# Gate columns placed anew around the S5 branch's outer products, V and states, and four blocks' sums of squares on another engine, in a decoder step on one Trainium2 core

## The chip, the cores and the metric

The kernel runs on one core of one Trainium2 chip. The metric is the time of one execution on the device in microseconds (us). TensorE is PE in the profile, its weight load PEld, VectorE is DVE, ScalarE is ACT, GpSimd is POOL, SyncE is SP.

## The reference, cut to what matters

One layer of a hybrid decoder is computed for 2048 prompt positions and for 8 sequences of 4 new positions each. Its first half is what matters here:

```python
xn = _rmsnorm(h, norm_mix[l])
proj = jnp.einsum('btd,de->bte', xn, w_in[l])          # 1024 -> 3072
u_pool = proj[..., :POOL_WIDTH]                        # 512
u_ssm = proj[..., POOL_WIDTH:POOL_WIDTH + SSM_WIDTH]   # 512
gates = jax.nn.sigmoid(proj[..., POOL_WIDTH + SSM_WIDTH:])   # 2 x 1024
a_out = _pool_mixer(hist[l], u_pool, ...)
y_ssm, s_re_last, s_im_last = _s5_mixer(u_ssm, ...)    # 32 groups, 64 complex states, a scan over time
z = jax.nn.gelu(y_ssm)
b_out = z * jax.nn.sigmoid(z @ glu_w + glu_b)
merged = gates[0] * (a_out @ w_branch_pool) + gates[1] * (b_out @ w_branch_ssm)
h = h + merged @ w_out
h = h + SwiGLU(RMSNorm(h))
```

## The kernel before, in words

All large products are made of three float16 matmuls for each pair of operands split into a high and a low part (`mm3`, lines 117 to 119). The projection's output is cut into chunks of 256 rows. A **column** is what one step of `chunk` issues: 24 matmuls for 128 output rows and 512 or 272 positions (five columns, three of 512 and two of 272, make 128 rows; ten make a chunk), ACT's evacuation out of PSUM (L363 or L366), and the DMA of the column before. Four PSUM buffers (`mm`) serve the columns, two others (`s5`) serve S5.

**`norm_in`** (from L198) normalizes the 17 blocks of input rows. `norm` takes the sum of squares of each row (L229, on ACT with a sum output), the inverse root on DVE (`rstd_of`, L61 to L72), and the split into high and low parts; `put_part` transposes these on PE (L137). Weight preparation stands beside it (`Win.prep`): a square on ACT (L89), a product on DVE (L96, or L92 where a column stands between), for the first weights two small matmuls (L98, L100), ten small DVE operations (L103 to L179) and eight splits (L52 on ACT, L53 on DVE). Blocks 0 and 1 are taken singly, blocks 2 and 3 together, and later blocks in pairs while the first columns run.

**The S5 stage** has four units of eight groups. `S5.run` is a generator; whatever it yields, a number n of columns is issued at that place (a bare yield is one). The order of instructions on each of PE, DVE, ACT and POOL is the program's here (`manual_schedule`). For each unit `un`:

- `states` (L686): for each of eight groups a matmul of V and U (L693) and two copies out of PSUM (L696), by ACT and by DVE, into R.
- `tmat` (L661): ACT copies TT into T (L666), DVE makes the outer products O (`outer`, L621: lines 626 and 629, three operations).
- `load` (L672): SP fetches the next unit's U.
- `vmat` of the next unit (L631): the outer products VT on DVE; eight transposes of VT (L641) in two PSUM buffers, each copied into V by ACT (L642); eight small matmuls (L645) whose result ACT copies into M (L648); DVE adds the diagonal into M (L383, `m<-m,dd`); SP stores M into TT.
- `scan` (L709): a scan over time of R, all on DVE (L705, L707, L737), with eight columns between its parts.
- `outputs` (L750): DVE and ACT fill S (L759, L761, L757); then columns; then for each group two matmuls (L766 with T, L767 with S) and ACT's copy into Y (L768), in two halves of four groups with a column behind each, one more column at the end, and the store of Y.

Each column of a chunk also carries a step of the preparation of the next chunk's weights, by its number k in the chunk: 1 the square, 3 the product and POOL's maximum, 7 the ten small operations, 8 and 9 four splits each (for the first chunk, 0 to 4 finish chunk 1, 5 to 9 are for the next).

Behind S5, Pool takes 13 columns, `Branch.weights` 5, then 4; the first GLU tile's preparation is issued, 5 more columns, the GLU's matmuls and all columns that are left (`put(100)`); then `merge_tile` runs for eight tiles, with the next tile's GLU issued after four of its eight steps. There the framework's scheduler orders the instructions, and it lays Pool's matmuls in the midst of columns. 100 columns exist in all.

Of the kernel before, what the change touches and what calls it, by code (L numbers as in the profile page):

```python
# [13 lines left out]
AF = mybir.ActivationFunctionType  # L14
OP = mybir.AluOpType
# [40 lines left out]
def rstd_of(E, ss, n, w=128):  # L56

    nc = E.nc
    t = E.small.tile([128, 4, n], F32, tag=f"rs{n}", name="rs")
    v, y, a, h = (t[:w, i] for i in range(4))  # L60
    nc.vector.tensor_scalar(v, ss, 1.0 / D, EPS, op0=OP.mult, op1=OP.add)  # L61
    nc.vector.tensor_scalar(h, ss, -0.5 / D, -0.5 * EPS, op0=OP.mult, op1=OP.add)  # L62
    nc.vector.tensor_scalar(a.bitcast(I32), v.bitcast(I32), 1, None, op0=OP.logical_shift_right)  # L63
    nc.vector.tensor_scalar(y.bitcast(I32), a.bitcast(I32), -1, 0x5F3759DF, op0=OP.mult, op1=OP.add)  # L64
    for _ in range(3):
        if n == 1:
            nc.vector.tensor_scalar(a, y, y, h, op0=OP.mult, op1=OP.mult)  # L67
            nc.vector.tensor_scalar(y, a, 1.5, y, op0=OP.add, op1=OP.mult)  # L68
            continue
        nc.vector.tensor_tensor(a, y, y, op=OP.mult)  # L70
        nc.vector.tensor_tensor(a, a, h, op=OP.mult)
        nc.vector.scalar_tensor_tensor(y, a, 1.5, y, op0=OP.add, op1=OP.mult)  # L72
    return y
# [67 lines left out]
class Win:  # L141


    def __init__(self, E, ctx, w_in, g):
# [7 lines left out]
        self.wp = ctx.enter_context(E.tc.tile_pool(name="wpart", bufs=3))  # L152
        self.R, self.W = {}, {}

    def load(self, c, half=None):
        if c not in self.R:
            self.R[c] = self.raw.tile([128, KB, 256], F32, name="wr")
        n = slice(0, 256) if half is None else slice(half * 128, half * 128 + 128)
        w = self.w[:, c * 256:(c + 1) * 256].rearrange("(k p) f -> p k f", p=128)
        self.E.nc.sync.dma_start(self.R[c][:, :, n], w[:, :, n])  # L160

    def prep(self, c, ps=None, half=None):

        E, nc, t = self.E, self.E.nc, self.R[c]
        if c not in self.W:
# [32 lines left out]
def norm_in(E, ps, win, x_p, x_s, xh, xl, u_d, s5):  # L198

    nc, tc = E.nc, E.tc  # L200
    with ExitStack() as ctx:
        ld = ctx.enter_context(tc.tile_pool(name="xld", bufs=5))
        wk = ctx.enter_context(tc.tile_pool(name="xwk", bufs=2))
        X = {}
# [18 lines left out]
        def norm(bs):  # L223

            w = BLK[bs[0]][1]
            ss = E.small.tile([128, len(bs)], F32, tag=f"ss{len(bs)}", name="ss")
            for i, b in enumerate(bs):
                sq = wk.tile([128, D], BF16, name="sq", bufs=1)
                nc.scalar.activation(sq[:w], X[b][:w], AF.Square, accum_out=ss[:w, i:i + 1])  # L229
            yield  # L230
            r = rstd_of(E, ss[:w], len(bs), w)
            rs = E.small.tile([128, len(bs)], F32, tag=f"rx{len(bs)}", name="rx")
            nc.vector.tensor_scalar(rs[:w], r, SX, None, op0=OP.mult)
            yield
            for i, b in enumerate(bs):
                hi, lo = norm_parts(E, wk, X.pop(b), w, rs[:w, i:i + 1])
                n0 = BLK[b][0]
                T[b] = [partial(put_part, E, ps, nc.scalar.copy, hi, w, xh, n0, "tp"),
                        partial(put_part, E, ps, nc.vector.tensor_copy, lo, w, xl, n0, "s5")]
                yield  # L240
# [37 lines left out]
        g, w = norm([0]), win.prep(2, ps, 0)  # L278
# [9 lines left out]
        g, w = norm([1]), win.prep(2, ps, 1)  # L288
# [10 lines left out]
        g, w = norm([2, 3]), win.prep(3, ps)  # L299
# [12 lines left out]
        w = None  # L312
        for p in range(8):
            bs = [2 * p + 4, 2 * p + 5] if p < 6 else [16] if p == 6 else []
            nb = [b for b in (2 * p + 2, 2 * p + 3) if p and b < 16]
            g = norm(bs) if bs else iter(())
# [11 lines left out]
            n0, w = (p * 256, 256)  # L328
            if p == 7:
                w = 288  # L330
# [115 lines left out]
class S5:  # L446
# [184 lines left out]
    def vmat(self, un):  # L631
        E, nc, ps, mp = self.E, self.E.nc, self.ps, self.mats
        G = slice(un * 8, un * 8 + 8)
        VT = mp.tile([128, 8, L, HD], F32, name="vt", tag="vt")
        self.outer(VT, self.PV[:, :, :, G], self.BT[:, :, G])
        yield 2 if un < 3 else 1
        V = mp.tile([128, 8, 128], F32, name="v5")
        for h in range(2):
            p = ps.tile([128, 512], F32, name="mm", tag="s5", bufs=2)
            for g in range(4):  # L640
                nc.tensor.transpose(p[:, g * 128:(g + 1) * 128], VT[:, h * 4 + g].rearrange("p j h -> p (j h)"), E.id32)  # L641
            nc.scalar.copy(V[:, h * 4:h * 4 + 4].rearrange("p g m -> p (g m)"), p)  # L642
        p = ps.tile([128, 512], F32, name="mm", tag="s5", bufs=2)
        for g in range(8):
            nc.tensor.matmul(p[:, g * HD:(g + 1) * HD], VT[:, g].rearrange("p j h -> p (j h)"),  # L645
                             self.CT[:, 0, un * 8 + g], start=True, stop=True)
        M = mp.tile([128, 8, HD], F32, name="m5")
        nc.scalar.copy(M.rearrange("p g h -> p (g h)"), p[:, :128])  # L648
        dd = mp.tile([128, 8, HD], F32, name="dd")
        hi = slice(96, 128)  # L650
        tt(E, dd[hi], self.dv[hi, G][:, :, None].to_broadcast([32, 8, HD]),
           E.id32[hi, None, 112:128].to_broadcast([32, 8, HD]), OP.mult)
        tt(E, M[hi], M[hi], dd[hi], OP.add)
        TT = mp.tile([128, L, 8, HD], F32, name="tt5", tag="vt")
        nc.gpsimd.memset(TT, 0.0)
        for t in range(L):
            nc.sync.dma_start(TT[0:HD * (t + 1), t], M[HD * (L - 1 - t):128])
        self.M[un] = (V, TT)
        yield 0
# [26 lines left out]
    def states(self, un):  # L686

        E, nc, ps, wk = self.E, self.E.nc, self.ps, self.wk
        V, U = self.M[un][0], self.U[un]
        R = [wk.tile([128, 4, UC], F32, name=f"r{i}") for i in range(2)]  # L690
        for g in range(8):
            p = ps.tile([128, 512], F32, name="mm", tag="s5", bufs=2)
            nc.tensor.matmul(p[:, :UC], V[:, g], U[:, g], start=True, stop=True)  # L693
            e = (g % 2) * 64
            for i in range(2):
                (nc.vector.tensor_copy if i else nc.scalar.copy)(R[i][e:e + 64, g // 2], p[i * 64:i * 64 + 64, :UC])  # L696
        return R

    def cmul_add(self, un, k, o, x, a):
# [50 lines left out]
    def outputs(self, un, a):  # L750
        E, nc, ps, wk = self.E, self.E.nc, self.ps, self.wk
        pr = slice(un * 4, un * 4 + 4)
        T, O = self.M.pop(un)
        U = self.U.pop(un)
        S = wk.tile([128, 8, YC], F32, name="st5")
        nc.gpsimd.memset(S[:, :, 0:1], 0.0)
        nc.scalar.copy(S[:, :, NC:], self.S0[:, un * 8:un * 8 + 8])  # L757
        for i in range(2):
            nc.vector.tensor_copy(self.fin[:, i, 0, pr], a[i][:, :, NC - 1])  # L759
            for e in range(2):  # L760
                nc.vector.tensor_copy(S[i * 64:i * 64 + 64, e::2, 1:NC], a[i][e * 64:e * 64 + 64, :, 0:NC - 1])  # L761
        yield (3, 2, 2, 4)[un]
        Y = wk.tile([128, 8, YC], F32, name="y5")
        for g in range(8):
            p = ps.tile([128, 512], F32, name="mm", tag="s5", bufs=2)
            nc.tensor.matmul(p[:, :YC], T[:, g].rearrange("p t h -> p (t h)"), U[:, g, :YC], start=True, stop=False)  # L766
            nc.tensor.matmul(p[:, :YC], O[:, g].rearrange("p t h -> p (t h)"), S[:, g], start=False, stop=True)  # L767
            nc.scalar.copy(Y[:, g], p[:, :YC])  # L768
            if g % 4 == 3:
                yield  # L770
        nc.vector.tensor_reduce(self.ymx[:, un:un + 1], Y.rearrange("p g c -> p (g c)"), axis=AX.X, op=OP.max,
                                apply_absolute_value=True)
        o = self.y_d.offset + un * 128 * NT
        dst = lambda c, n: bass.AP(tensor=self.y_d.tensor, offset=o + c, ap=[[NT, HD], [HD * NT, 8], [1, n]])
        for t in range(L):
            nc.sync.dma_start(dst(t * NC, NC), Y[HD * t:HD * t + HD, :, 0:NC])
            if t < 4:
                nc.sync.dma_start(dst(NP_ + 8 * t, 8), Y[HD * t:HD * t + HD, :, NC:])
        yield
# [18 lines left out]
    def run(self):  # L798
        self.U = {}
        self.load(0)  # L800
        yield from self.vmat(0)
        for un in range(4):
            R = self.states(un)
            yield min(un, 1)
            yield from self.tmat(un)
            if un < 3:
                self.load(un + 1)
                yield from self.vmat(un + 1)
            yield from self.scan(un, R)
            yield from self.outputs(un, R)  # L810
        self.finish()
        yield
# [1030 lines left out]
```

## Time and profile before

| | us |
|---|---|
| median of 3 runs (2407.16 to 2411.3) | 2409.38 |
| the profiled execution's own time | 2412.55 |
| its span, first to last instruction | 2410.5 |
| PE busy | 2297.5 |
| DVE busy | 1657.8 |
| ACT busy | 1027.0 |

The mean granted clock of TensorE over the span is 0.982 of full speed (2.4 GHz). A row of the timeline gives start and length in us, the engine, the line, the operation and its tiles (out<-in), and in brackets the time that the engine sat idle before it and what ended that.

### The profile page before, as it was taken

Reading aid. Unit: us, or ns where it says so; the run is one execution under the profiler, and the core shown is the slowest. Engines: PE = TensorE matmul, PEld = TensorE weight load, DVE = VectorE, ACT = ScalarE, POOL = GpSimd, SP = SyncE. Lnnn points to the kernel's source line nnn. Section 1 sums busy time; section 2 is a strip of 40 time slices with the busy share of each in tenths; the row PEclk is TensorE's granted clock in tenths of the full one; section 3 lists DMA queues with packets and bytes.
Section 4 is the critical chain, followed back from the end, with each engine's and each line's share of the span. In section 5 each row is a group of like instructions: output and inputs, shape, how many; then the busy total and the mean of one; then the engine's idle time right before and its main releaser. Section 6 shows DMA issues by size and latency. Waiting matters only on the chain. (4 is left out here: it accounts for less than half of the span.)

```text
span 2410.5 us, 43285 instructions
## 1 busy us (share of the span) xinstructions
PE 2297.5 (95%) x16971; PEld 1616.3 (67%) x16971; DVE 1657.8 (69%) x4011; ACT 1027.0 (43%) x1867; POOL 384.5 (16%) x428
## 2 busy tenths in 40 slices
PE   6989999999999999997999999999999989988998
PEld 5866555555678874555888888888888754433543
DVE  6757757838568778776555565555555688789877
ACT  6633232244334433455445454444454552243332
POOL 0000000000000000000121121211121345454342
PEclk8999999999999999998999999999999999999999
DMA  6232332255334343323122121221222344444332
GB/s 208 81 91 81 76 99 76 76 165 185 127 112 130 111 132 137 140 75 123 54 80 79 63 80 54 80 88 54 80 70 72 119 144 159 135 170 142 123 125 79
DMA packets 200529, 257.50 MB, mean 107 GB/s; under 512 B 23798, under 2 KB 161334, under 8 KB 199805
## 3 DMA queue, kind: packets, MB, share of 16 engines
q1 hardware_dynamic: 179813, 228.73, 30.6%
q10 hardware_dynamic: 20480, 25.83, 3.0%
q8 instruction: 132, 2.16, 0.4%
q14 instruction: 72, 0.59, 0.1%
q0 software_dynamic: 32, 0.18, 0.0%
HBM read 167.03 MB, written 86.67 MB: 105 GB/s over the span
## 5 line engine op out<-in xcount | busy, mean ns | idle before, releaser
L974 PEld LDWEIGHTS <-W 128*128 128x128 f16 x7392 | 726.0, 98 | 115.8 <-issue 15.6
L974 PE MATMUL p<-m,W 128*128 128x256 f16 (+1 forms) x3084 | 356.6, 275 | 1.5 <-ACT v L1006 1.5
L118 PE MATMUL mm<-xl,wh 128*128 128x512 f16 (+4 forms) x1072 | 348.2, 325 | 1.6 <-DVE xl L138 1.6
L117 PE MATMUL mm<-xh,wh 128*128 128x512 f16 (+4 forms) x1072 | 348.3, 325 | 0.0
L119 PE MATMUL mm<-xh,wl 128*128 128x512 f16 (+4 forms) x1072 | 348.0, 325 | 0.0
L117 PE MATMUL pd<-m,W 128*128 128x512 f16 x616 | 235.4, 382 | 19.2 <-ACT xr L1222 5.5
L119 PE MATMUL pd<-m,W 128*128 128x512 f16 x616 | 234.5, 382 | 1.6 <-DVE W L383 1.6
L118 PE MATMUL pd<-m,W 128*128 128x512 f16 x616 | 235.2, 382 | 0.0
L974 PE MATMUL p<-x,W 128*128 128x256 f16 x1848 | 205.7, 273 | 3.6 <-ACT p L995 2.8
L974 PE MATMUL p<-xq,W 128*128 128x256 f16 x1764 | 199.8, 275 | 5.5 <-ACT p L995 4.1
L1007 POOL TENSOR_TENSOR p<-v,p 128x256 f32<-128x256 f32 (+1 forms) x88 | 71.3, 811 | 668.2 <-ACT v L1006 522.9
L383 DVE TENSOR_TENSOR w<-u,p 128x272 f32<-128x272 f32 (+1 forms) x86 | 36.5, 424 | 172.6 <-PE p L974 169.3
L119 PEld LDWEIGHTS <-wl 128*128 128x128 f16 x1072 | 106.8, 100 | 68.6 <-issue 3.1
L118 PEld LDWEIGHTS <-wh 128*128 128x128 f16 x1072 | 106.9, 100 | 66.4 <-issue 0.6
L117 PEld LDWEIGHTS <-wh 128*128 128x128 f16 x1072 | 107.4, 100 | 65.3 <-issue 0.6
L1220 POOL TENSOR_TENSOR xq<-xq,xr 128x512 f32<-128x512 f32 x90 | 128.7, 1450 | 42.0 <-DVE xq L1221 17.3
L366 ACT ACTIVATE go<-mm,wc 128x512 f32<-128x512 f32 (+1 forms) x80 | 48.3, 604 | 181.8 <-PE mm L119 176.5
L118 PEld LDWEIGHTS <-W 128*128 128x128 f16 x616 | 60.5, 98 | 93.1 <-issue 22.7
L119 PEld LDWEIGHTS <-W 128*128 128x128 f16 x616 | 60.6, 98 | 76.2 <-DVE W L383 2.8
L117 PEld LDWEIGHTS <-W 128*128 128x128 f16 x616 | 60.6, 98 | 74.1 <-issue 2.2
L1006 ACT COPY v<-p 128x272 f32<-128x272 f32 (+1 forms) x86 | 32.1, 374 | 168.0 <-PE p L974 160.9
L117 PE MATMUL po<-woh,m 128*128 128x512 f16 x256 | 97.0, 379 | 0.9 <-DVE x L383 0.9
(474 smaller groups left out, 4404.2 us busy)
## 6 DMA issues: line engine op xcount, KB each, us to landing
f_d<-m SPq DMA_DIRECT2D x44, 512.0 KB, 3.3
xq<-f_d SPq DMA_DIRECT2D x40, 512.0 KB, 4.5
x<-in_x_prompt_dram SPq DMA_DIRECT2D x32, 512.0 KB, 4.5
xq<-h_d SPq DMA_DIRECT2D x32, 512.0 KB, 4.1
g<-g_d SPq DMA_DIRECT2D x56, 256.0 KB, 2.8
g_d<-go ACTq DMA_DIRECT2D x48, 256.0 KB, 2.0
gr<-in_ffn_w_gate_dram SPq DMA_DIRECT2D x23, 512.0 KB, 4.2
ur<-in_ffn_w_up_dram SPq DMA_DIRECT2D x23, 512.0 KB, 5.1
```

The lines of the kernel that those rows point to most:

```text
L117: nc.tensor.matmul(q, ah, bh, start=first, stop=False)
L118: nc.tensor.matmul(q, ah, bl, start=False, stop=False)
L119: nc.tensor.matmul(q, al, bh, start=False, stop=last)
L366: nc.scalar.activation(o[:, :w], q[:, :w], AF.Tanh, scale=cc[:, 1:2])
L383: E.nc.vector.tensor_tensor(o, a, b, op=op)
L974: nc.tensor.matmul(q, W[:, x, a, ka], X[b][:, y, k, :w], start=begin and k == v == 0, stop=end and k == 3 and v == 2, skip_group_check=True)
L1006: nc.scalar.copy(v, x)
L1007: nc.gpsimd.tensor_tensor(p5, v, p5, op=OP.add)
L1220: add = (lambda o, x: tt(E, o, o, x, OP.add)) if end else (lambda o, x: nc.gpsimd.tensor_tensor(o, o, x, op=OP.add))
```

## The change

In `vmat` three columns instead of two (one in the last unit) stand between the outer products and V's transposes, and a new column stands between V's copies and the matmuls of L645. `states` becomes a generator with a column after its fourth group; the column that stood behind the states of units 1 to 3 goes. In `outputs` 2, 1, 2 and 4 columns instead of 3, 2, 2 and 4 stand ahead of the matmuls of Y in units 0 to 3. In `norm_in` the sums of squares of blocks 0 to 3 are taken by DVE, as a product of the block with itself with a sum output, instead of by ACT.

```diff
             for i, b in enumerate(bs):
                 sq = wk.tile([128, D], BF16, name="sq", bufs=1)
-                nc.scalar.activation(sq[:w], X[b][:w], AF.Square, accum_out=ss[:w, i:i + 1])
+                if b < 4:
+                    nc.vector.scalar_tensor_tensor(sq[:w], X[b][:w], 1.0, X[b][:w], op0=OP.mult, op1=OP.mult,
+                                                   accum_out=ss[:w, i:i + 1])
+                else:
+                    nc.scalar.activation(sq[:w], X[b][:w], AF.Square, accum_out=ss[:w, i:i + 1])
...
         self.outer(VT, self.PV[:, :, :, G], self.BT[:, :, G])
-        yield 2 if un < 3 else 1
+        yield 3
...
             nc.scalar.copy(V[:, h * 4:h * 4 + 4].rearrange("p g m -> p (g m)"), p)
+        yield 1
         p = ps.tile([128, 512], F32, name="mm", tag="s5", bufs=2)
...
                 (nc.vector.tensor_copy if i else nc.scalar.copy)(R[i][e:e + 64, g // 2], p[i * 64:i * 64 + 64, :UC])
+            if g == 3:
+                yield 1
         return R
...
-        yield (3, 2, 2, 4)[un]
+        yield (2, 1, 2, 4)[un]
...
         for un in range(4):
-            R = self.states(un)
-            yield min(un, 1)
+            R = yield from self.states(un)
             yield from self.tmat(un)
```

## Rows read from the trace of the kernel before

**Rows 1.** The page's part 1: busy us (share of the span) and instructions.

```profile
PE 2297.5 (95%) x16971; PEld 1616.3 (67%) x16971; DVE 1657.8 (69%) x4011; ACT 1027.0 (43%) x1867; POOL 384.5 (16%) x428
```

**Rows 2.** Busy time by stage; columns: stretch, us, five engines' busy, clock, DMA, GB/s.

```profile
142.40:508.40 366.00, 345.84 (x1854) 204.09 (x1853) 255.96 (x976) 113.81 (x230) 8.47 (x23) 0.97 0.32 86
...
680.50:900.00 219.50, 211.43 (x1875) 183.83 (x1873) 174.46 (x393) 97.44 (x173) 1.08 (x3) 0.99 0.42 123
```

**Rows 3.** Waits of PE in the S5 stage: us in total, times, longest.

```profile
PE mm L693 <- DVE r L696: 6.2, 10, 2.1
PE mm L645 <- ACT v L642: 3.1, 3, 2.5
PE mm L693 <- DMA u<-u_d: 3.0, 1, 3.0
...
PE mm L766 <- ACT y L768: 2.3, 2, 1.2
```

**Rows 4.** Timeline of PE: states of unit 1, V, S of unit 2, states of unit 3.

```profile
253.65 1.20 PE L693 MATMUL mm<-u,v 128*128 128x272 f32 x4 [0.60 <-DVE r L696]
...
270.88 1.28 PE L641 MATMUL mm<-id,vt 128*128 128x128 f32 x8 [1.94 <-DVE vt L629]
...
404.25 0.79 PE L767 MATMUL mm<-st,o 128*128 128x264 f32 x2 [2.84 <-DVE st L761]
...
429.04 1.20 PE L693 MATMUL mm<-u,v 128*128 128x272 f32 x4 [2.13 <-DVE r L696]
```

**Rows 5.** Busy time of two stretches, with the granted clock in the third last place.

```profile
271.60:278.40 6.80, 6.78 (x27) 4.61 (x25) 3.12 (x15) 1.38 (x3) 0.96 (x1) 0.50 0.66 99
...
158.95:165.80 6.85, 6.51 (x12) 3.17 (x12) 2.22 (x5) 1.89 (x5) 0.00 (x0) 0.50 0.35 82
```

**Rows 6.** Timeline of ACT: a square of the preparation, evacuations of three neighbouring columns.

```profile
385.67 1.90 ACT L89 ACTIVATE wh<-wr 128x2048 bf16<-128x2048 f32 x1
...
393.05 0.49 ACT L366 ACTIVATE go<-mm,wc 128x272 f32<-128x272 f32 x1 [2.09 <-DMA g_d<-go]
...
395.82 0.49 ACT L366 ACTIVATE go<-mm,wc 128x272 f32<-128x272 f32 x1 [2.10 <-PE mm L119]
...
401.00 0.69 ACT L366 ACTIVATE go<-mm,wc 128x512 f32<-128x512 f32 x1 [4.69 <-PE mm L119]
```

**Rows 7.** Groups of DVE in S5, shapes apart: count, busy us, mean ns, idle.

```profile
L629 DVE TENSOR_TENSOR vt<-vt,t 128x1024 f32<-128x1024 f32 x4 | 4.9, 1225 | 0.1
```

**Rows 8.** Timeline of DVE in unit 1, from the addition into M to S.

```profile
276.11 0.29 DVE L383 TENSOR_TENSOR m<-m,dd 32x128 f32<-32x128 f32 x1 [3.47 <-ACT m L648]
...
306.10 0.15 DVE L103 TENSOR_SCALAR pr<-pr 128x1 f32<-128x1 f32 x1
...
307.63 0.14 DVE L179 TENSOR_SCALAR wc<-pw 128x1 f32<-128x1 f32 x1
...
315.75 1.67 DVE L53 SCALAR_TENSOR_TENSOR wl<-wr,gs,wh 128x256 f16<-128x256 f32 x4
...
319.02 1.41 DVE L761 COPY st<-r 64x1020 f32<-64x1020 f32 x2
```

**Rows 9.** The tail: timeline of DVE, and L117's instructions (first and last start).

```profile
632.70 1.28 DVE L53 SCALAR_TENSOR_TENSOR zl<-y,bk,zh 128x1024 f16<-128x1024 f32 x1
...
656.08 0.48 DVE L53 SCALAR_TENSOR_TENSOR bl<-bt,bk,bh 128x256 f16<-128x256 f32 x1 [0.58 <-ACT bh L52]
...
661.91 0.69 DVE L1504 SCALAR_TENSOR_TENSOR y<-gq,y 128x512 f32<-128x512 f32 x1 [0.69 <-ACT gq L1503]
...
667.05 1.28 DVE L53 SCALAR_TENSOR_TENSOR zl<-y,bk,zh 128x1024 f16<-128x1024 f32 x1 [1.22 <-ACT zh L52]
...
L117 PE MATMUL mm<-zh,gluh x128: 269/273/448, 648.6 to 865.5; 128*128 128x256 f16 x112, 128*128 128x288 f16 x16
```

**Rows 10.** Timeline of DVE at the start of `norm_in`.

```profile
18.56 0.16 DVE L96 TENSOR_TENSOR pr<-pr,gmx 128x1 f32<-128x1 f32 x1 [1.39 <-ACT wh L89]
...
31.08 0.16 DVE L96 TENSOR_TENSOR pr<-pr,gmx 128x1 f32<-128x1 f32 x1 [3.84 <-ACT wh L89]
```

## The prediction, made before the result was known

> **What bounds the kernel now.** I read the page's busy times first: TensorE (PE) is busy for 95% of the span and no other engine passes 70% [rows 1]. So the table by stage comes next, to find where PE is not busy. In the S5 stage it misses 20.2 us of 366, in the merge stage 8.1 of 219.5 [rows 2]. The table of waits then names what PE waits for inside S5: the state copies 6.2, V 3.1, the load of U 3.0, S 2.8, the copies of Y 2.3 [rows 3], and PE's timeline shows each in its place [rows 4]. Last, the granted clock: after several of these waits it falls from 2.4 to 1.2 GHz, as in the 6.8 us behind the wait of 1.94 [rows 5]. The matmuls are the same before and after. The time therefore changes by PE's waits and half-clock stretches alone, and a column is worth something only as cover: one of 512 takes 5.18 us, one of 272 2.78 (evacuations of neighbouring columns start that far apart, [rows 6]).
>
> **Where the columns go.** I numbered the columns by the generator's steps. A column n has 272 positions when n mod 5 is 3 or 4, and weight preparation of the next chunk hangs on n mod 10 (1: a square on ACT; 3: a reduction; 7: ten small DVE operations; 8 and 9: four splits each on ACT and DVE). The change issues 74 columns in S5 instead of 66. Between V's last matmul (L645) and the first Y of units 0 to 3 stood 11, 10 and 10 columns, and in unit 3, which prepares no V, 13 behind the states; now it is 10, 9, 10 and 12.
>
> **V: a gain of 12 us.** V's transposes get three columns instead of two or one behind the outer products, and L645 gets one behind the copies of V. The outer products are two sets of three operations of 1.22 [rows 7], so they end some 8 us after the last state copy; the three columns last 10.7 to 15.5, so the wait of 1.94 goes [rows 4], and the copies of V, which made PE wait 3.1 in all [rows 3], lie beside the new column. That is 5.5 with two small waits for vt. A half-clock stretch goes with each of the two large ones: 6.8 us at 0.50 with PE busy for 6.78 of them [rows 5] have lost 3.4. I take 6.4 for both, since V's transposes were through before.
>
> **U: a gain of 5 us.** The first states now come two columns (7.96 us) later, past U's landing: 3.0 idle [rows 3], and the states behind that wait no longer run at half clock (0.50 over 6.85 us, [rows 5]). Those would lose 3.4, but the copies set the pace of part of them; estimate 2.0.
>
> **States: a loss of 2.6 us.** A half of four groups waits once, about 0.6, where eight groups wait three times [rows 4]; that saves 0.6 in each of four units. But what stands in ACT's and DVE's queues ahead of the copies matters more. Unit 3 of before shows it: its last column ahead of the states has n mod 10 of 8, and with four splits (1.67 on DVE, [rows 8], as much on ACT) in front of the copies the wait is 2.13 instead of 0.5 [rows 4]. The new placement puts splits ahead of the second half of unit 0 and of both halves of unit 2, and a square of 1.9 (the row at L89, [rows 6]) ahead of unit 1's first half: 3 x 1.6 + 2.0 = 6.8 against the 1.6 that goes from unit 3. Net 5.2 lost, 2.6 after the saving.
>
> **S: a loss of 11 us, the largest term.** DVE works in order, and the scan is written behind the addition into M, which waits for L645 (3.47 idle, [rows 8]). In unit 1 from that addition at 276.11 to the last copy into S at 320.43 DVE took 44.3, of which 1.6 were the ten small operations and 1.6 the splits [rows 8]: the bare chain is 41.1, and 40.4 to the part that the first Y needs (the last copy of 0.7 is for another). The addition starts 0.34 after L645. Now the cover after the change. Unit 0: 6 x 5.18 + 4 x 2.78 = 42.2, and 0.45 for Y's first matmul; preparation 1.7, chain 0.34 + 40.4 + 1.7 = 42.4: about even, 0.5 lost because splits stand ahead of the copy of M. Unit 1: 5 x 5.18 + 4 x 2.78 = 37.0, and 0.45; preparation is 1.6 + 1.6 + 1.6 + 0.1 = 4.9, the chain 45.6: PE waits 8.1. Unit 2: 42.2 against 45.5, as before, where the same count gives the measured wait of 2.84 [rows 4]; it stays. Unit 3: 6 x 5.18 + 6 x 2.78 = 47.8, and 0.45, against 1.1 to the last state copy, 3.6 for one set of outer products, 40.1 and 3.3 of preparation = 48.1: even. So 8.6 more idle, and behind the wait of 8 the half clock, which loses up to 3.4 in a stretch like those of [rows 5] and half of that in a shorter one: I take 2.5.
>
> **Y: nothing.** The waits for Y's copies (2.3, [rows 3]) come from squares ahead of them. They go, and splits ahead of three other halves cost about 1.0 each.
>
> **New half-clock stretches: a loss of 3 us.** The four lengthened state waits are of 2.1 to 2.6. Of two such waits before, 1.94 was followed by half clock and 2.13 was not. At even odds and some 1.7 each that is 3, between 0 and 7.
>
> **The tail: a loss of 4 us.** Pool and Branch take 13, 5, 4 and 5 columns as before, so the eight columns come off the end: the seven behind the first GLU matmuls, 26.6 us, are gone, and one of the five ahead of them. From the pool's end 13 columns remain, 53 us; zl stood ready at 634.0 [rows 9], 46 us after the pool's end at 588, so the first GLU still does not wait. But the seven columns hid the last bl, which ends 8.0 after the GLU's start at 648.6, and the second tile's zl, 19.7 after it [rows 9]. Without them PE has the GLU (48 matmuls of 256, 5.2 at the rate of a column of 272) and, before the second GLU, four merges (24 each, 10.5). If nothing else is put there, PE waits 1.4 for bl and some 6 for zl, since DVE must also do four merges. This part is ordered by the framework's scheduler, which can put the next four merges first; then 1 to 2 stay. I take 4, with 0 and 8 as ends.
>
> **Squares on DVE: nothing.** DVE stood idle for 1.39 and 3.84 us ahead of L96 [rows 10], exactly where the squares of block 1 and of blocks 2 and 3 now lie. No row shows a DVE multiply with a sum output; the nearest, the multiply of two f32 tiles over 512 elements, took 0.69 [rows 9], so about 1.25 for 1024. Block 1: the square ends when ACT's square did, with ACT's own next square a microsecond earlier, so L96 stays within 0.1. Blocks 2 and 3: 2.5 into 3.84 idle. Block 0 runs before the weights land. I take 0, with -0.3 and +0.5 as ends. The Trainium skill (Vector Engine (DVE) Microarchitecture Reference, section 7, Points that are easy to get wrong) says that this operation with two sources in SBUF that are not bf16 runs at half throughput; the row of 0.69 for 512 f32 elements speaks against it here. By the rule the four squares would take an estimated 2.3 each, and the sum would be 1.8 us worse.
>
> **The sum.** Against the profiled execution (2412.55, its span 2410.5): 12 + 5 - 2.6 - 11 - 3 - 4 = -3.6, so 2416.2. That execution is 3.2 above the median of 2409.38; against the median it is 2413. A measurement of this kernel tells about 0.2% (4.8 us) from no change.
>
> **The rivals.**
> Faster: the scan does not wait in unit 1. The gain of 17 at V and U is in the rows, and the loss at S is counted, not seen. If DVE's chain there ended within the cover, say because M's addition came earlier than I place it, 10 us of loss fall away, and with a tail of 2: 2409.4 - 9 = about 2400. For it speaks that units 0 and 3 come out even within half a microsecond; against it that the same count reproduces all waits for S of before.
> Slower: the second GLU tile. The place is zl of the second tile; if the scheduler holds the order GLU after four merges, as all the later tiles have it, PE waits 7.5 in all and the clock falls behind it (up to 3.4): 11 instead of 4, 2420. It decides from the point at which zl comes more than 10.5 us after the GLU's end; alone it came 14.4 after. With the other end of the half-clock term 2424.
> No effect: the gains are eaten earlier than I think and the scheduler fills the tail: 2409, within 2.
>
> **How the numbers follow.** The forecast of 2413 gets 0.42 (its own range 2409 to 2418), the faster rival 0.20, the slower 0.25, no effect 0.13. Of the forecast two thirds lie within 4.8 us of the median, the rest above it. So faster 0.19, same 0.41, slower 0.40. The range reaches from the faster rival to just short of the slower one's end: 2400 to 2423.
>
> **What would show it.** Right: the waits of L645 for v and of L641 for vt gone; the wait of L693 for U gone; a new wait of L767 for S near 8 us in unit 1 and one near 2.8 in unit 2; waits of L693 of 2 us where splits or a square stand ahead; merge beginning right behind the first GLU with a wait for zl in the second; L96 at 18.6 and 31.1 or a little earlier. Wrong: no wait of several microseconds for S in unit 1, or a merge stage without a wait for the second zl (then faster), or more than one wait above 5 us in the tail (then slower).

## The result, and the profile after

| | before | after |
|---|---|---|
| median, us | 2410.13 (4 runs on the same chip) | 2426.16 (4 runs, 2424.36 to 2429.42) |
| ratio, 95% interval | 1 | 1.007 (1.0058 to 1.0083) |
| span of the profiled execution | 2410.5 | 2423.3 |

The change costs 0.7%, or 16 us between the medians and 12.8 between the two spans. All four runs lie above the range of 2400 to 2423. The matmuls are the same in number, and PE's busy time has hardly moved (the page's first part, of the kernel after, against [rows 1]):

```profile
PE 2297.0 (95%) x16971; PEld 1617.0 (67%) x16971; DVE 1659.8 (68%) x4019; ACT 1022.3 (42%) x1859; POOL 382.4 (16%) x428
```

So the loss shows as idle time of PE. The same table by stage as in [rows 2] (stretch, its length, busy us of PE, PEld, DVE, ACT, POOL, clock, DMA), for the S5 stage and for the stage from the first GLU to Out's first product:

```profile
142.40:552.30 409.90, 378.64 (x2043) 221.54 (x2042) 257.28 (x982) 119.84 (x240) 8.50 (x24) 0.97 0.30 82
681.00:913.50 232.50, 217.00 (x1922) 188.57 (x1921) 182.71 (x409) 107.18 (x190) 1.07 (x3) 0.99 0.42 121
```

The S5 stage misses 31.3 us of PE instead of 20.2. From its first column to its last four small matmuls, which stand ahead of its last column, it now holds eight columns more, six of 512 and two of 272 positions, 36.6 us by the prediction's prices; this stretch grew by 44.3 (365.6 to 409.9), so 7.6 are lost there. From S5's end to the first matmul of the merge (from 508.05 to 680.51 before, from 552.29 to 696.18 after, by PE's timeline) the 172.5 us of before became 143.9 with those eight columns fewer: 8.1 lost. The merges up to Out took 2.0 less and everything behind them 0.9 less. 7.6 + 8.1 - 2.0 - 0.9 = 12.8, the whole difference of the spans.

PE's waits by what ended them (us in total, times, longest), kernel after; ahead of the dots in 142 to 520, against [rows 3], behind them in 520 to 920:

```profile
PE mm L698 <- DVE r L701: 11.7, 8, 2.5
PE mm L774 <- DVE st L768: 11.7, 3, 8.0
PE mm L773 <- ACT y L775: 3.3, 2, 2.6
...
PE mm L117 <- ACT bt L1531: 7.7, 2, 7.1
PE mm L773 <- ACT y L775: 4.5, 1, 4.5
PE mm L117 <- ACT zh L52: 3.6, 3, 2.2
```

(L698 is L693 of before, L773 and L774 are L766 and L767, L775 is the copy into Y, L701 the copy into R, L1531 the GLU's tanh.) The waits for v, vt and u are gone. In their place stand r with 5.5 more than before, S with 8.9 more, y with 5.5 more in the two stretches together, and in the tail a wait of 7.1 for bt that the kernel before does not have. Three of them on PE's timeline: S in unit 1, Y in unit 3, the first GLU.

```profile
342.12 1.22 PE L774 MATMUL mm<-st,o 128*128 128x264 f32 x2 [8.03 <-DVE st L768]
...
528.43 1.25 PE L773 MATMUL mm<-u,t 128*128 128x264 f32 x2 [4.50 <-ACT y L775]
...
690.91 0.37 PE L117 MATMUL mm<-zh,gluh 128*128 128x256 f16 x1 [7.08 <-ACT bt L1531]
```

A stretch at half clock goes with each of the three (0.50 is 1.2 GHz); each begins while PE still waits:

```profile
336.31:346.55 10.24, 4.43 (x10) 3.53 (x11) 7.73 (x29) 0.76 (x2) 0.00 (x0) 0.50 0.00 0
527.46:534.29 6.83, 5.86 (x14) 3.48 (x15) 1.18 (x3) 1.95 (x6) 0.00 (x0) 0.50 0.41 154
687.88:694.71 6.83, 3.80 (x19) 2.69 (x19) 4.00 (x6) 4.63 (x7) 0.00 (x0) 0.50 0.39 110
```

The wait for S is the one predicted. The other two are not, and the trace proposes a cause for each.

**Y.** ACT waits ahead of the copies into Y. Its rows in unit 3, and DVE's just before:

```profile
521.42 1.41 DVE L768 COPY st<-r 64x1020 f32<-64x1020 f32 x2
522.86 0.15 DVE L103 TENSOR_SCALAR pr<-pr 128x1 f32<-128x1 f32 x1
...
524.18 0.23 DVE L176 TENSOR_SCALAR gs<-gmix,pw 128x8 f32<-128x8 f32 x1
```

```profile
524.45 0.51 ACT L52 ACTIVATE wh<-wr,gs 128x256 f16<-128x256 f32 x1 [4.55 <-DVE gs L176]
...
526.43 1.69 ACT L52 ACTIVATE wh<-wr,gs 128x256 f16<-128x256 f32 x4
528.02 0.63 ACT L775 COPY y<-mm 128x264 f32<-128x264 f32 x2
```

The columns ahead of unit 3's Y now have the numbers 66 to 69, so the ten small operations (step 7) and both sets of splits (8 and 9) fall among them. These columns are issued behind the scan. The ten operations therefore stand on DVE behind the last copy into S (521.42, from there L103 at 522.86), ACT's first split waits 4.55 for their result gs, and the column's evacuation and the first Y copies stand behind that split on ACT. In unit 0 the same pair costs ACT 3.0 and PE 2.65.

**The first GLU.** ACT's order in the tail:

```profile
682.00 0.72 ACT L52 ACTIVATE ah<-a,bk 128x512 f16<-128x512 f32 x1 [3.19 <-DMA a<-a_d]
...
686.47 0.72 ACT L52 ACTIVATE ah<-a,bk 128x512 f16<-128x512 f32 x1 [3.18 <-DMA a<-a_d]
...
688.41 1.99 ACT L52 ACTIVATE woh<-br,pw 128x2048 f16<-128x2048 f32 x1
...
690.30 1.01 ACT L1531 ACTIVATE bt<-mm,glub,bk 128x256 f32<-128x256 f32 x2
```

PE issues the GLU at 681.04; its first tanh runs at 690.30, behind the second tile's two copies ah and a split of Out's weights (woh, 1.99). Each of the two copies waits 3.2 for a load, since the halves of a_out share one buffer. The kernel before has seven columns behind the first GLU, and the kernel after has none.

### The profile page after: what moved, and what is told of

Same layout as the page of the kernel before. It is cut to its first block, busy times and chain, and to the rows that moved or that the text cites. A ratio compares the mean times of both kernels' runs of the same rounds, so it can differ in the third digit from the quotient of the medians.

```text
span 2423.3 us, 43283 instructions
## 1 busy us (share of the span) xinstructions
PE 2297.0 (95%) x16971; PEld 1617.0 (67%) x16971; DVE 1659.8 (68%) x4019; ACT 1022.3 (42%) x1859; POOL 382.4 (16%) x428
## 3 DMA queue, kind: packets, MB, share of 16 engines
q8 instruction: 132, 2.16, 0.4%
## 5 line engine op out<-in xcount | busy, mean ns | idle before, releaser
L117 PE MATMUL mm<-xh,wh 128*128 128x512 f16 (+4 forms) x1072 | 348.4, 326 | 0.0
L117 PE MATMUL pd<-m,W 128*128 128x512 f16 x616 | 236.4, 384 | 17.7 <-DVE xr L1227 7.8
L117 PEld LDWEIGHTS <-wh 128*128 128x128 f16 x1072 | 107.2, 100 | 65.6 <-issue 1.3
L117 PEld LDWEIGHTS <-W 128*128 128x128 f16 x616 | 60.9, 99 | 74.3 <-issue 3.0
L1012 ACT COPY v<-p 128x272 f32<-128x272 f32 (+1 forms) x86 | 32.1, 373 | 167.6 <-PE p L980 160.7
L117 PE MATMUL po<-woh,m 128*128 128x512 f16 x256 | 97.0, 379 | 0.9 <-DVE x L387 0.9
```

Of the source, the lines that this page charges most:

```text
L117: nc.tensor.matmul(q, ah, bh, start=first, stop=False)
L1012: nc.scalar.copy(v, x)
```

## Experiments

Each has its own runs of the kernel before on the same chip, 7 to 14 per batch (medians 2409.91, 2410.90, 2411.02). Stages are compared by the traces. An edit that adds or takes out lines shifts the line numbers behind it by a few; the tiles name the operation.

**1. The two halves of the change.** DVE's squares alone, on the kernel before:

```diff
-                nc.scalar.activation(sq[:w], X[b][:w], AF.Square, accum_out=ss[:w, i:i + 1])
+                if b < 4:
+                    nc.vector.scalar_tensor_tensor(sq[:w], X[b][:w], 1.0, X[b][:w], op0=OP.mult, op1=OP.mult,
+                                                   accum_out=ss[:w, i:i + 1])
+                else:
+                    nc.scalar.activation(sq[:w], X[b][:w], AF.Square, accum_out=ss[:w, i:i + 1])
```

> The kernel before with the squares of blocks 0 to 3 on DVE alone. Theory A (all of the 16 us is PE's waits around the moved columns): no change, 2410 within 2, the first column of S5 starting at 142.4 as before. Rival B (the squares are a part of the loss, at half throughput on DVE as a page of the Trainium skill has it): 2412 or more, with L96 of block 1 at 19.5 instead of 18.6 and that of blocks 2 and 3 at 31.9.

Measured: 2409.26, ratio 0.9999 (0.9990 to 1.0009). DVE's timeline of this kernel:

```profile
17.22 1.22 DVE L230 SCALAR_TENSOR_TENSOR sq<-x 128x1024 bf16<-128x1024 f32 x1
18.36 0.08 DVE L230 DVE_READ_ACCUMULATOR sq<-x 128x1 f32 x1
18.36 0.15 DVE L96 TENSOR_TENSOR pr<-pr,gmx 128x1 f32<-128x1 f32 x1
...
30.45 0.16 DVE L96 TENSOR_TENSOR pr<-pr,gmx 128x1 f32<-128x1 f32 x1 [0.81 <-ACT wh L89]
```

A square takes 1.22 us, and L96 comes at 18.36 and 30.45 where it came at 18.56 and 31.08 [rows 10]. The first column of S5, expected at 142.4, starts at 143.04; in the runs below it starts anywhere from 141.5 to 143.5, with and without the squares, so this tells nothing. The squares cost nothing that can be measured. The other half, the change without the squares:

> The changed kernel with the squares back on ACT. Theory A: 2426 within 2, all waits of the changed kernel in place (S of unit 1 near 8.0, Y of unit 3 near 4.5, the first GLU near 7.7). Rival B: 2422 or less.

Measured: 2428.28, ratio 1.0075 (1.0060 to 1.0090), with the waits of the kernel after (S 11.7, r 11.7, y 7.8, bt 8.1). The columns are the whole loss, as near as these runs can tell.

**2. Y: the ten small operations moved.** In chunks behind the first, step 5 instead of 7 issues them, so that they no longer stand in the columns ahead of Y in units 0 and 3:

```diff
-                        if k in (1, 3, 7, 8, 9) if i else k > 4:
+                        if k in (1, 3, 5, 8, 9) if i else k > 4:
```

> The changed kernel with the ten small DVE operations of the next chunk's preparation at the sixth column of a chunk instead of the eighth. Theory A (in units 0 and 3 ACT stands in splits that wait for these ten operations, which stand behind the whole scan on DVE, and Y's copies stand behind the splits): the ten operations move into or ahead of the scan, the waits for Y's copies in unit 3 (4.5, and its half clock, some 3) and in unit 0 (2.65) fall to about 1 each, S comes 1.6 later in units 0 and 3 and 1.6 earlier in unit 1 (8.0 to 6.4); in sum 5 to 8 us faster than the changed kernel, 2418 to 2421. Rival B (Y's copies wait for the splits themselves, not for what these wait for): Y's waits stay, 2425 or more.

Measured: 2418.99, ratio 1.0036 (1.0023 to 1.0049), 7 us less than the kernel after. Waits in 142 to 520:

```profile
PE mm L774 <- DVE st L768: 11.8, 3, 6.5
PE mm L698 <- DVE r L701: 11.7, 8, 2.5
PE mm L773 <- ACT y L775: 0.7, 1, 0.7
```

Behind 520 PE does not wait for y any more. It waits 1.2 ahead of unit 3's first matmul with S; the profile puts this down to a split (wh), but the copy into S that this matmul reads ends just then (519.9), behind the ten operations. The waits for y fall from 7.8 to 0.7 and the stage from 409.9 to 400.1 (its profile is of the fastest of five runs, and S5 runs at half clock for 17.1 us instead of 27.3; the stretch of 6.8 behind Y's wait is gone). S of unit 1 falls to 6.5, because there the operations no longer stand within the cover; S of unit 0 rises to 2.5, because there they now do. The cause of the waits for Y is the place of the ten operations behind the scan.

**3. S: one column of cover given back to unit 1,** taken from amid its states:

```diff
-            if g == 3:
+            if g == 3 and un != 1:
                 yield 1
...
-        yield (2, 1, 2, 4)[un]
+        yield (2, 2, 2, 4)[un]
```

> The changed kernel, with unit 1's column amid the states issued ahead of its Y instead (2 columns there, as in the kernel before); the number of columns stays. Theory (cover): one more column of 5.18 between the matmuls of L650 and Y takes the wait for S in unit 1 from 8.0 to about 2.8, and some of the half clock behind it; the states of unit 1 keep about 3 of waits. 6 to 9 less: 2417 to 2420. Rival (the scan starts later by as much as the column moves, so that the wait is not a matter of cover): the wait stays near 8, the time near 2426.

Measured: 2419.09 (2415.54 to 2426.86, 6 runs), ratio 1.0032 (1.0020 to 1.0044). PE's timeline of this kernel:

```profile
339.13 1.22 PE L774 MATMUL mm<-st,o 128*128 128x264 f32 x2 [2.85 <-DVE st L768]
```

The wait for S falls by 5.18, from 8.03 to 2.85: the length of the column to the hundredth. The profiled execution (span 2425.1) is the longest of this kernel's six and shows nothing of the gain in its length: its S5 stage takes 410.4. It has more half clock there, 34.1 us with PE busy for 32.1, against 27.3 with 20.5 in the kernel after. Half of the busy time is lost (at 0.50 the kernel before starts the matmuls of 512 positions 0.43 apart from 276.42 on, at full clock 0.22 apart), so 5.8 more, about what the waits shrank by (5.6). One of these stretches stands behind the same wait for y in unit 0 (2.64) behind which the kernel after ran on at full clock:

```profile
246.20:249.60 3.40, 3.40 (x14) 2.15 (x14) 0.00 (x0) 0.55 (x2) 0.00 (x0) 0.50 0.00 0
```

The wait is settled by the trace, the 7 us by the median.

**4. The states in one piece,** every column with its number kept:

```diff
-            if g == 3:
-                yield 1
+        yield 1
         return R
```

> The changed kernel, with the column amid the states issued behind all eight groups instead; every column keeps its number. Theory (two halves pay twice for splits and squares ahead of the copies): the waits for r fall from 11.7 to about 7.6 (three of 0.5 in each unit, 1.6 for the splits ahead of unit 2), and 1 to 3 of half clock with them: 2420 to 2423. Rival (the split of the states is worth its column, since a half waits once where a whole waits three times): the waits for r stay near 12 or rise, 2426 to 2428.

Measured: 2419.01, ratio 1.0035 (1.0021 to 1.0049). The waits for r fall from 11.7 only to 9.8: the wait behind a square in unit 1 stayed at 2.49, where I had expected 0.5. Still the gain is 7 us, more than either theory gave. The trace shows where it came from:

```profile
522.64 0.71 PE L772 MATMUL mm<-u,t 128*128 128x264 f32 x2 [0.91 <-ACT y L774]
```

Y of unit 3 waits 0.91 instead of 4.50. Unit 3 prepares no V, so its cover begins with its last state. A column amid the states is one column less behind them; with it behind, the scan and the ten operations end earlier against Y. This I had not thought of. Beside that, the half-clock stretches of S5 add up to 13.7 us in this trace instead of 27.3.

**5. V: the new column undone,** set ahead of V's transposes instead:

```diff
-        yield 3
+        yield 4
...
-        yield 1
         p = ps.tile([128, 512], F32, name="mm", tag="s5", bufs=2)
```

> The changed kernel with V's new column undone: the column between V's copies and the matmuls of L650 stands ahead of V's transposes instead (four there); every column keeps its number, and U's load keeps its cover. Theory (the term of V in the sum): PE waits for v again, about 2.5 in each of the two units where four splits stand ahead of the copies on ACT and 0.4 in the two others, with half-clock stretches behind the longer ones: 3 to 8 more, 2429 to 2434. Rival (the copies of V were hidden anyway, or the wait only moves into S, which is late in any case): 2425 to 2427, and the waits for S fall by as much as those for v rise.

Measured: 2428.56, ratio 1.0076 (1.0061 to 1.0091), not told apart from the kernel after (1.0058 to 1.0083). PE waits for v again, 4.2 in all:

```profile
162.74 1.51 PE L649 MATMUL mm<-ct,vt 128*128 128x16 f32 x12 [1.77 <-ACT v L646]
...
198.32 1.93 PE L649 MATMUL mm<-ct,vt 128*128 128x16 f32 x9 [1.82 <-ACT v L646]
...
248.41 0.71 PE L772 MATMUL mm<-u,t 128*128 128x264 f32 x2 [0.86 <-ACT y L774]
```

But in unit 0 the wait for S (0.88) is gone, that for y falls from 2.65 to 0.86, and r in all falls by 0.8; the stage is 0.9 longer. Each of the two waits above is followed by 6.8 us at half clock, but other stretches of the stage are missing in this trace (23.9 us in all, against 27.3). The time lies just between the theory's 2429 and the rival's 2427 and does not decide. The waits speak for the rival, though not only at S: in unit 0 most of the time gained at v was waited for again at S and Y. The four splits that the moved column carries stand on ACT ahead of V's copies here (196.09 and 197.70); in the kernel after they stand behind these and ahead of the copy of M (196.97 and 198.59), behind which the scan begins.

**6. The tail.** First a try that moves columns from ahead of the GLU to behind it (4 and 5 become 1 and 0):

```diff
-        put(4)
+        put(1)
...
-        put(5)
+        put(0)
```

> The changed kernel with eight columns less ahead of the first GLU tile (3 and 5 of them less at the two places), so that seven stand behind it again as in the kernel before. Theory A (the first GLU waits because its tanh on ACT stands behind copies that wait for DMAs, where no columns are left to lie beside it): the wait of 7.1 and its half clock and the wait for the second zl go, 8 to 11 us faster than the changed kernel, 2415 to 2418. Rival B (the tail only passes on a lateness of the S5 stage: the GLU's inputs come late by as much as S5 does): the wait stays or moves to the merges, 2424 or more.

Measured: 2428.01, ratio 1.0078 (1.0061 to 1.0095). The wait for bt is gone and another has come, in the midst of a column:

```profile
670.81 0.58 PE L117 MATMUL mm<-zh,gluh 128*128 128x256 f16 x2 [6.23 <-ACT zh L52]
```

From S5's end to the merge 142.4 us pass, against 143.9. In either placement ACT makes zh at about 670 (669.6 here, 670.5 in the kernel after), so the shift exchanged one wait for another. The time is the rival's, and for zh its reason holds too: zh comes 39.3 later than in the kernel before (630.3), and S5 ends 43.5 later. Then the wait of ACT itself, by a second buffer for the halves of a_out:

```diff
-            a = wk.tile([128, 2, w], F32, name="a", tag="a", bufs=1)
+            a = wk.tile([128, 2, w], F32, name="a", tag="a", bufs=2)
```

> The changed kernel, with two buffers instead of one for the halves of a_out in the GLU tile's preparation. Theory (ACT's order): the first GLU waits 7.1 us for its own tanh because that stands on ACT behind the second tile's two copies ah, and these wait 3.2 each for a load that can start only when the one buffer is free. With two buffers the loads run ahead: the wait falls to 2 or less, the half-clock stretch behind it goes or shrinks, merge starts 5 to 8 us earlier, 2418 to 2421. Rival (the GLU is late by its own chain, tanh, bt, split, or by the weights of Out): the wait for bt stays near 7, the time at 2426.

Measured: 2418.62, ratio 1.0029 (1.0017 to 1.0041). ACT's timeline of this kernel, the second tile's copies and the first tanh:

```profile
676.30 0.72 ACT L52 ACTIVATE ah<-a,bk 128x512 f16<-128x512 f32 x1 [4.18 <-DMA a<-a_d]
...
677.50 0.71 ACT L52 ACTIVATE ah<-a,bk 128x512 f16<-128x512 f32 x1
...
682.99 1.01 ACT L1531 ACTIVATE bt<-mm,glub,bk 128x256 f32<-128x256 f32 x2
```

The last copy ah comes at 677.50 instead of 686.47, the tanh at 682.99 instead of 690.30. PE waits 2.0 for bt in all, the half-clock stretch ahead of the merge is gone, and S5's end to the merge takes 136.2 instead of 143.9. With the eight columns' 36.6 that is within 0.4 of the kernel before: 7.7 of the tail's 8.1 were this wait and the clock behind it. The split of Out's weights stands ahead of the tanh here too (1.99 at 681.10), so it was not the cause.

**7. The parts put together.** V's columns and the squares kept; no column amid or behind the states, none behind the store of Y, one more ahead of each Y; step 5:

```diff
-            if g == 3:
-                yield 1
+        yield 0
...
-        yield (2, 1, 2, 4)[un]
+        yield (3, 2, 3, 5)[un]
...
                 nc.sync.dma_start(dst(NP_ + 8 * t, 8), Y[HD * t:HD * t + HD, :, NC:])
-        yield
...
-                        if k in (1, 3, 7, 8, 9) if i else k > 4:
+                        if k in (1, 3, 5, 8, 9) if i else k > 4:
```

> The changed kernel with V's columns and DVE's squares kept; no column amid or behind the states, none behind the store of Y, and instead 3, 2, 3 and 5 columns ahead of Y; the ten small operations of weight preparation at step 5 instead of 7. S5 issues 70 columns. Theory (each term of the sum as measured): waits for r near 6 in all, for S none above 2, for y none above 1.3, for v, vt and u none; the stage loses 15 to 20 instead of 37 in the kernel before and 45 in the changed one. The tail has four columns less than before and loses about 4. Together 2393 to 2400, faster than both. Rival (the terms do not add, because a wait that is closed comes back at the next copy): S5 loses 30 or more, 2408 or above.

Measured: 2396.28, ratio 0.9940 (0.9927 to 0.9952). Waits in 142 to 520:

```profile
PE mm L698 <- DVE r L701: 6.3, 12, 0.8
PE mm L773 <- DVE st L767: 2.7, 1, 2.7
PE mm L772 <- ACT y L774: 2.1, 3, 1.2
```

The stage takes 364.2, with four columns more than before (18.3): 19.7 gained. Only the wait for S in unit 1 came out larger than expected (2.7 against 2). Up to the merge the tail loses 1.9. Then the second buffer for a_out's halves with it:

> The recombined kernel of the batch before (70 columns in S5, step 5) with two buffers for a_out's halves as well. Theory (ACT's order makes the GLU's waits in the tail): the wait of 2.2 for the first GLU's tanh and that of 1.8 for bh fall; 1 to 4 less, 2392 to 2395. Rival (with 18 columns left behind the preparation the order on ACT is no longer what decides): 2396.

Measured: 2390.17, ratio 0.9913 (0.9898 to 0.9927). That is below the 2392 to 2395 of the theory. The wait for bt (2.2) is gone, the one ahead of bh is 1.5 instead of 1.8, as good as unchanged. But from S5's end to the merge only 0.2 less pass, since Pool's waits for ao grew from 1.1 to 3.1; of the 4.4 between the two spans 2.2 lie in the merges, and their cause was not traced. Last, one more column ahead of unit 1's Y:

```diff
-        yield (3, 2, 3, 5)[un]
+        yield (3, 3, 3, 5)[un]
```

> The same with one more column ahead of unit 1's Y (3, 3, 3 and 5), 71 in S5. Theory (cover): the wait for S of 2.7 in unit 1 and the 3.4 us at half clock behind it go, 3 to 4.4 less than the kernel without it, while one column less in the tail costs up to 1: 2389 to 2393. Rival (a column more in S5 is a column less in the tail at its full price): no gain, 2392 to 2396.

Measured: 2384.84 (2383.0 to 2386.07), ratio 0.9889 (0.9873 to 0.9906), lower than expected. PE waits for S no more, and the S5 stage runs 71 columns with PE idle for 7.3 us:

```profile
141.90:505.80 363.90, 356.58 (x1971) 210.20 (x1969) 250.99 (x964) 114.90 (x230) 7.92 (x22) 0.99 0.31 86
```

It ends at 505.8, earlier than the kernel before with 66 columns (508.05), and up to the merge the tail loses nothing (0.4 less than before). This kernel is 1.1% faster than the one before and 1.8% faster than the changed one, by the two ratios. The second buffer was not run on the kernel before, so how much of the 1.1% it would give there alone is not known; without it the recombined kernel is 0.6% faster.

## Why the prediction was wrong, step by step

Of the two outer cases slower had the larger chance (0.40 against 0.19, with 0.41 for no change beyond the noise), but the forecast of 2413 and its range failed: the sum gave 3.6 us of loss between the profiled executions, and 12.8 were measured. The 9.2 between them are 8.0 in S5 (0.4 gain forecast, 7.6 loss measured) and 4.1 in the tail, less the 2.9 that merge and the rest gave back.

**S, the largest term: right.** 8.1 us forecast in unit 1 and 8.03 measured, 2.84 and 2.78 in unit 2, 0.5 and 0.88 in unit 0. The half clock that goes with it, 10.24 us with PE busy for 4.43, loses 2.2, where 2.5 were forecast. Experiment 3 shows the arithmetic of cover: one column of 5.18 takes 5.18 from the wait.

**V and U: the waits went, the gain is not theirs alone.** The waits for v, vt and u of [rows 3] and [rows 4] are gone as said. But the 12 us were counted as if PE could keep them. Experiment 5 undoes the column behind V's copies and nothing measurable is lost; in unit 0 S and Y had been waited for instead. The step that failed is the adding up: time gained ahead of the scan counts only where the cover behind it is long enough. This is shown for that column in unit 0; no run undoes the third column ahead of V's transposes, or the cover of U's load, alone. In the recombined kernel, which has that cover, whole states and the ten operations earlier, the stage does gain 19.7.

**States: right in each half, wrong in the balance.** The eight halves wait 0.83, 2.23, 2.49, 0.60, 2.16, 2.19, 0.60 and 0.60, where the prediction's prices (eight of 0.6, three of 1.6 more, one of 2.0 more) add up to 11.6 and 11.7 was measured. The saving was mis-sized: I took 0.6 in each of four units (2.4, so the sum there should have read 2.8 and not 2.6). In the kernel before the four units wait for r 0.2, 1.5, 1.5 and 3.1, the last 1.5 without its splits. Two halves of 0.6 save 0.3 in three units and lose 1.0 in unit 0, where the states stood behind U's wait and hardly waited for r: nothing is saved. So 5.5 more idle instead of 2.6. The lost column of cover in unit 3 (experiment 4) was missed.

**"Y: nothing": wrong, the step that failed most.** I had priced the splits ahead of Y by their own length, 1.0 each. What costs is what they wait for: the ten operations on DVE behind the scan. 5.5 us more idle, and 6.83 at half clock with the longer wait. Experiment 2, which moves only those ten, shows it. The sign stood in the trace of the kernel before, in unit 3:

```profile
481.83 0.51 ACT L52 ACTIVATE wh<-wr,gs 128x256 f16<-128x256 f32 x1 [5.51 <-DVE gs L176]
```

There ACT waits for gs behind the scan too, and PE lost nothing by it: two more columns without splits (60 and 61) stood between these splits and Y's first matmul, at 488.76. The change put splits into the last columns ahead of Y.

States and Y together are 8.4 more idle than forecast, against the 8.0 missing in S5. Of half clock in S5 8.4 gained and 5.5 lost were forecast, a net gain of 2.9. The traces show 23.9 us of it with PE busy for 23.6 before, and 27.3 with 20.5 after; with half of the busy time lost that is a net gain of 1.5. The 11.1 us more idle lengthened the stage by 7.6; 2.0 of the 3.5 between them are not traced.

**The tail: the right cause, the wrong wait.** That the eight columns come off the end, seven of them from behind the first GLU, was right, and 4 us of net loss came near the 5.2 that the stages show (8.1 less 2.9), but by luck: no wait of 6 for the second tile's zl came; its zh waits 2.2. I had followed what the second GLU needs and not what stands on ACT between the first GLU's matmuls and its own tanh. The second buffer (experiment 6) closes most of that wait, and the loss goes with it.

**The squares: right.** 1.22 us each with 1.25 estimated from the multiply of two f32 tiles. The estimate of 2.3 by the half throughput that the Trainium skill states (Vector Engine (DVE) Microarchitecture Reference, section 7, Points that are easy to get wrong) is not what this operation takes here: the row of 1.22 decides.

**The new half-clock stretches** behind state waits: 3 us forecast; two of 3.41 came, which lose 1.7 each.

The slower rival had nearly the right number (2420) for another reason; a second mechanism of the same kind, Y, was not among the rivals at all.

## What to carry to other kernels

Where engines run in program order, price a moved column by everything that hangs on it: an operation of 0.2 us put behind a long chain on one engine holds up the other engine that needs its result, and through it the engine that bounds the kernel. Count cover as columns between the start of a chain and its first reader, not as columns in a stage, and add up gains only where the next reader on the same chain is not late already. A column that is taken from the end is worth what stood beside it there, so look at the in-order queue of every engine that the uncovered matmuls need.

## What the hardware showed that I had not expected

The same wait at the same place is followed by half clock in one execution and not in another. In the kernel after, PE waits 2.65 for Y in unit 0 and runs on at full clock; in experiment 3, which issues the same instructions up to that point, the same wait of 2.64 is followed by 3.4 us at 0.50. The wait in the kernel after and, below it, in experiment 3:

```profile
245.94 0.71 PE L773 MATMUL mm<-u,t 128*128 128x264 f32 x2 [2.65 <-ACT y L775]
```

```profile
244.80 0.71 PE L773 MATMUL mm<-u,t 128*128 128x264 f32 x2 [2.64 <-ACT y L775]
```

The stretch of the kernel after, to be set beside that of experiment 3:

```profile
245.94:249.35 3.41, 3.40 (x22) 2.82 (x23) 0.21 (x1) 0.98 (x3) 0.00 (x0) 1.00 0.00 0
```

So a stretch at half clock behind this wait is a chance, not a fixed price, and two kernels whose waits differ by 5 us had profiles of nearly the same length (2423.3 and 2425.1).

A product of a 128 x 1024 f32 block with itself, with the sum output, took 1.22 us on DVE and 0.08 more to read the sum.
